# Layer-norm sums with the activations stationary and two columns of ones, and half of the output's stores on ScalarE's queue

## The chip, the cores and the metric

The kernel runs on one core of a Trainium2 chip. The metric is device microseconds (us) of one execution, median of several runs. Five engines share the core's memory: TensorE (PE in the profile; its weight loads are listed as PEld), VectorE (DVE), ScalarE (ACT), GpSimd (POOL) and SyncE (SP), which here only issues transfers. Each engine works through its own instructions in a fixed order and waits on semaphores for the others.

## The reference

Two layers of an encoder on 256 tokens of 2048 features. The first layer's mixer holds the convolution module whose layer norm is changed; the last operation of the program is an RMS norm whose result is stored.

```python
def layer_norm(x, g, b, eps=LN_EPS):
    mu = jnp.mean(xf, axis=-1, keepdims=True)
    var = jnp.mean(jnp.square(xf - mu), axis=-1, keepdims=True)
    y = (xf - mu) * lax.rsqrt(var + eps) * g.astype(jnp.float32) + b.astype(jnp.float32)
...
def conformer_conv(val, gate, dw, db, ln_g, ln_b):
    h = val * jax.nn.sigmoid(gate)
    h = depthwise_conv(h, dw, db)          # 31 taps, 1024 channels
    h = layer_norm(h, ln_g, ln_b)
    return jax.nn.silu(h)
...
    return jnp.concatenate([a_out, b_out], axis=-1) @ w_out
...
    return rms_norm(x, final_g)            # end of the program
```

The mean and the variance of a token run over the 1024 channels of the convolution.

## The kernel before

**The stream of weights.** Nearly the whole program is one stream of 960 weight tiles of 128x1024 f32 (512 KB). For each, SP loads `raw`, ScalarE rounds it to `hi` (L223), VectorE computes the rest `lo` (L225), and TensorE multiplies with both: `lin_ws` (L263, L264) holds the weights stationary, `lin_xs` (L298) holds the activations stationary. `raw` has four buffers, `hi` and `lo` three each, so that the conversion can run a few tiles ahead of TensorE and no more.

**Side work.** What isn't in that stream (the convolution, its layer norm, preparing the state-space parameters) is written as generators in `self.side`. After each weight tile `background` plays steps of the first generator as far as its credit goes: `self.rate` is added per tile, and each `yield` costs what it names. A generator that costs less ends after fewer tiles, and the next one starts sooner. `conv_ln` is followed by `s5_w1`: 32 rounds of six VectorE products (L865), with 1.5 MB of transfers each round by POOL's and SP's queues.

**The convolution's layer norm** lies with channels on partitions: `ac` is [128 channels, 8 groups, 256 tokens]. To sum over channels, a 128x128 matrix of ones is the stationary operand (`lhsT`) and `ac` moves through in eight matmuls of 256 columns (L537): every row of `pm` then holds the sums of all 256 tokens, already spread over the 128 partitions. The same is done with the squares (L545). The mean, the variance and the three Newton steps of the reciprocal root (`rsqrt_steps`) are therefore done on 128x256 tiles. Then ScalarE applies Silu (L555) and the result is split into `ao` for the output projection.

**Where it runs.** The program text has all eight attention heads first, then `mem_kv(0)`, whose weight tiles play `conv_ln`. A scheduler that simulates the program in time decides the final order on each engine; so the heads, the weight tiles of `mem_kv(0)` and the steps of the layer norm stand interleaved. PSUM tiles for small products come from two tags of two buffers, "ps" and "pt"; `pst` gives them in turn where no tag is named. In a tag, a new tile waits until the tile two before it in program order is read. The heads name theirs: scores on "ps"; `ps_wT`, `ps_o` and `ps_oT` on "pt".

**`bcast_rows`** (L140 to L146) makes a row [128, 256] out of a value per token: VectorE scales the identity by it (`dg`, L144, twice 128x128), TensorE multiplies ones with `dg` (L145, twice 128x128), VectorE copies the result (L146).

**The end.** In `ffn(1)`, L713 to L730, the two halves of 128 tokens (`tb`) are finished one after the other: sum of squares, reciprocal root, and four slices of 512 features, scaled on VectorE (slices 0 and 3, L729 and L725) or on ScalarE (1 and 2, L727), each stored by SP (L730).

Of the kernel before, what the change touches and what calls it, by code (L numbers as in the profile page):

```python
# [12 lines left out]
F32 = mybir.dt.float32  # L13
F32R = mybir.dt.float32r
I32 = mybir.dt.int32
AF = mybir.ActivationFunctionType
ALU = mybir.AluOpType
# [5 lines left out]
NTOK = 256  # L23
# [6 lines left out]
LN_EPS = 1e-5  # L30
# [4 lines left out]
class Build:  # L35
# [485 lines left out]
    def conv_ln(self, hp, ac, cdw, cv, tmp):  # L521

        nc, S = self.nc, self.S
        mu, rln, lni, lnt = tmp
        for ct in range(8):
            nc.vector.tensor_scalar(ac[:, ct, :], hp[:, ct, 0:NTOK], cdw[:, ct, 0:1], cv[:, 0, ct : ct + 1], op0=ALU.mult, op1=ALU.add)
            yield 0.4
            for j in range(1, 31):
                nc.vector.scalar_tensor_tensor(ac[:, ct, :], hp[:, ct, j : j + NTOK], cdw[:, ct, j : j + 1], ac[:, ct, :], op0=ALU.mult, op1=ALU.add)  # L529
                yield 0.4  # L530
        half = [slice(0, 4), slice(4, 8)]
        sh = [128, 4, NTOK]
        pm = self.pst("ps_ln")
        pv = pm[:, NTOK:]
        pm = pm[:, :NTOK]
        for ct in range(8):
            nc.tensor.matmul(pm, lhsT=self.ones, rhs=ac[:, ct, :], start=ct == 0, stop=ct == 7)  # L537
        nc.vector.tensor_scalar(mu, pm, 1.0 / 1024, None, op0=ALU.mult)
        sq = S.tile([128, 8, NTOK], F32, tag="A0", name="sq")
        for h in half:  # L540
            nc.vector.tensor_tensor(ac[:, h], ac[:, h], mu.unsqueeze(1).broadcast_to(sh), op=ALU.subtract)
            nc.scalar.activation(sq[:, h], ac[:, h], AF.Square)
            yield 1.2
        for ct in range(8):
            nc.tensor.matmul(pv, lhsT=self.ones, rhs=sq[:, ct, :], start=ct == 0, stop=ct == 7)  # L545
        nc.vector.tensor_scalar(mu, pv, 1.0 / 1024, LN_EPS, op0=ALU.mult, op1=ALU.add)
        yield from self.rsqrt_steps(rln, mu, lni.bitcast(I32), lnt, 1.2)
        ao = self.ao = S.tile([128, 2, 8, NTOK], F32R, tag="A0", name="ao")
        for h in half:
            nc.vector.tensor_tensor(ac[:, h], ac[:, h], rln.unsqueeze(1).broadcast_to(sh), op=ALU.mult)  # L550
            yield 1.1
        for ct in range(0, 8, 2):
            c2 = slice(ct, ct + 2)
            for i in range(ct, ct + 2):
                nc.scalar.activation(ac[:, i, :], ac[:, i, :], AF.Silu, bias=cv[:, 2, i : i + 1], scale=cv[:, 1, i : i + 1])  # L555
            self.split(ao[:, 0, c2], ao[:, 1, c2], ac[:, c2])
            yield 0.6
# [86 lines left out]
    def ffn(self, layer):  # L644
        nc, a, M, S = self.nc, self.a, self.M, self.S
# [66 lines left out]
        for tb in range(2):  # L712
            x = self.xslice(3)[tb]  # L713
            nc.vector.tensor_tensor(x, x, ps[tb], op=ALU.add)
            junk = self.R.tile([128, 512], F32, tag="junk", name="junk", bufs=1)
            nc.scalar.activation(junk, x, AF.Square, accum_out=self.ss[:, tb, 3:4])
            v = self.R.tile([128, 1], F32, tag="fv", name="fv")
            r = self.R.tile([128, 1], F32, tag="fr", name="fr")
            nc.vector.tensor_reduce(v, self.ss[:, tb], axis=AX.X, op=ALU.add)
            nc.vector.tensor_scalar(v, v, 1.0 / D, RMS_EPS, op0=ALU.mult, op1=ALU.add)  # L720
            self.rsqrt(r, v, [128, 1], "fs")
            for n in range(4):
                x = self.xslice(n)[tb]
                if n == 3:
                    nc.vector.scalar_tensor_tensor(x, x, r, fg[:, 1536:2048], op0=ALU.mult, op1=ALU.mult)  # L725
                elif n:
                    nc.scalar.activation(x, x, AF.Copy, scale=r)  # L727
                else:
                    nc.vector.tensor_scalar(x, x, r, None, op0=ALU.mult)  # L729
                nc.sync.dma_start(self.out[tb, :, n * 512 : n * 512 + 512], x)  # L730


    def s5_params(self):
# [535 lines left out]
```

## Time and profile before

| what | us |
|---|---|
| median of 3 runs (2898.27 to 2898.61) | 2898.45 |
| the profiled execution | 2897.15 |
| its span in the trace | 2895.0 |
| TensorE busy | 2854.1 (99%) |
| VectorE busy | 2203.7 (76%) |
| ScalarE busy | 1492.3 (52%) |

Busy time of TensorE is the union of its matmuls, whose ends are modelled: two matmuls that follow each other overlap in the listing, so the cost of one in a row of many is the distance of their starts and not their duration. The profiled execution is 2.15 us longer than its span, which is launch and end around it. "idle before" is time in which an engine had nothing running, followed by what ended it.

### The profile page before, as it was taken

How to read it: one execution, taken by the hardware profiler on the slowest of the kernel's cores; microseconds unless marked ns; L12 is line 12 of the kernel's file. 1: busy time of each engine (PE TensorE's matmuls, PEld its weight loads, DVE VectorE, ACT ScalarE, POOL GpSimd, SP SyncE). 2: the span in 40 equal slices, each digit the busy share in tenths (PEclk: the TensorE clock that was granted, in tenths of full speed). 3: DMA queues.
4: the chain of work that ended last, by engine and by line, in shares of the span. 5: the costliest groups of instructions: out<-in, count | busy, mean ns of one | idle time of the engine just before them, and what ended most of it. 6: DMA issues, size and time to landing. Idle time of an engine off the chain costs nothing. (4 is left out here: it accounts for less than half of the span.)

```text
span 2895.0 us, 44267 instructions
## 1 busy us (share of the span) xinstructions
PE 2854.1 (99%) x16673; PEld 2411.6 (83%) x16673; DVE 2203.7 (76%) x3524; ACT 1492.3 (52%) x2015; POOL 265.3 (9%) x504
## 2 busy tenths in 40 slices
PE   8999999999999999999999999999999999999998
PEld 7888887888888888888886787788888888888887
DVE  8899987877899887889855994556567776467765
ACT  6455554454555543455544544555455555345543
POOL 1000112222210102020201021000000000000000
PEclk9999999999999999999999999999999999999999
DMA  8655669978986788777887787655455555555554
GB/s 292 230 176 195 203 223 320 300 247 286 300 298 233 243 276 267 250 256 233 281 286 282 271 338 273 211 189 182 163 193 193 189 190 190 195 189 189 187 192 160
DMA packets 207143, 678.34 MB, mean 234 GB/s; under 512 B 33521, under 2 KB 36337, under 8 KB 206417
## 3 DMA queue, kind: packets, MB, share of 16 engines
q1 hardware_dynamic: 178592, 598.17, 61.1%
q0 software_dynamic: 28192, 76.83, 8.0%
q8 instruction: 130, 2.13, 0.3%
q14 instruction: 85, 0.69, 0.1%
q10 hardware_dynamic: 144, 0.52, 0.1%
HBM read 624.67 MB, written 61.08 MB: 237 GB/s over the span
## 5 line engine op out<-in xcount | busy, mean ns | idle before, releaser
L225 DVE TENSOR_TENSOR lo<-raw,hi 128x1024 fp32r<-128x1024 f32 x960 | 1173.1, 1223 | 534.6 <-ACT hi L223 530.9
L223 ACT CAST hi<-raw 128x1024 fp32r<-128x1024 f32 x960 | 1008.5, 1051 | 964.4 <-PE ps_xs L298 429.0
L263 PE MATMUL ps_ws<-x,hi 128*128 128x512 f32 x4352 | 1350.7, 396 | 8.0 <-DVE x L177 7.4
L264 PEld LDWEIGHTS ps_ws<-x,lo 128*128 128x128 f32 x4352 | 793.3, 188 | 191.4 <-DVE lo L225 14.8
L264 PE MATMUL ps_ws<-x,lo 128*128 128x256 f32 x4352 | 846.2, 280 | 8.1 <-DVE lo L225 7.7
L263 PEld LDWEIGHTS ps_ws<-x,hi 128*128 128x128 f32 x4352 | 674.3, 189 | 21.9 <-DVE x L177 7.4
L298 PE MATMUL ps_xs<-hi,hb 128*128 128x512 f32 x1328 | 356.5, 389 | 0.0
L298 PEld LDWEIGHTS ps_xs<-hi,hb 128*128 128x128 f32 x1328 | 249.1, 188 | 51.8
L298 PE MATMUL ps_xs<-lo,hb 128*128 128x512 f32 x664 | 204.8, 390 | 0.0
L298 PE MATMUL ps_xs<-hi,x 128*128 128x512 f32 x640 | 177.3, 394 | 1.9 <-ACT hi L223 1.9
L872 POOL DMA_DIRECT2D w1s<-d_pw x256 | 122.4, 486 | 589.5 <-DVE w1s L865 271.6
L298 PEld LDWEIGHTS ps_xs<-lo,hb 128*128 128x128 f32 x664 | 124.4, 188 | 25.9
L298 PEld LDWEIGHTS ps_xs<-hi,x 128*128 128x128 f32 x640 | 119.1, 188 | 31.6 <-issue 5.5
L298 PE MATMUL ps_xs<-hi,oT 128*128 128x512 f32 x512 | 141.1, 392 | 0.8 <-ACT hi L223 0.8
L298 PE MATMUL ps_xs<-hi,gT 128*128 128x512 f32 x512 | 138.1, 391 | 0.3 <-ACT hi L223 0.3
L271 ACT COPY z<-ps_ws 128x512 f32<-128x512 f32 x88 | 51.6, 587 | 145.2 <-PE ps_ws L263 145.2
L298 PEld LDWEIGHTS ps_xs<-hi,gT 128*128 128x128 f32 x512 | 95.6, 188 | 21.1 <-issue 0.8
L676 ACT ACTIVATE c<-z,fdb,fdw 128x256 f32<-128x256 f32 x176 | 96.3, 595 | 30.5 <-DVE z L671 30.4
L298 PEld LDWEIGHTS ps_xs<-hi,oT 128*128 128x128 f32 x512 | 95.3, 188 | 20.1 <-ACT hi L223 1.0
L529 DVE SCALAR_TENSOR_TENSOR av<-hpt,cdw,av 128x256 f32<-128x256 f32 x240 | 109.9, 484 | 0.7
L272 DVE TENSOR_TENSOR z<-ps_ws,z 128x512 f32<-128x512 f32 x88 | 60.7, 690 | 56.0 <-ACT z L271 55.7
L298 PE MATMUL ps_xs<-lo,x 128*128 128x512 f32 x320 | 100.8, 394 | 0.0
(288 smaller groups left out, 2582.0 us busy)
## 6 DMA issues: line engine op xcount, KB each, us to landing
raw<-ffn_w_up SPq DMA_DIRECT2D x352, 512.0 KB, 3.6
raw<-ffn_w_down SPq DMA_DIRECT2D x176, 512.0 KB, 4.3
raw<-xa_wv SPq DMA_DIRECT2D x64, 512.0 KB, 4.1
raw<-xa_wk SPq DMA_DIRECT2D x64, 512.0 KB, 4.4
raw<-xa_wq SPq DMA_DIRECT2D x64, 512.0 KB, 4.3
raw<-xa_wo SPq DMA_DIRECT2D x64, 512.0 KB, 3.7
raw<-ab_w_in SPq DMA_DIRECT2D x63, 512.0 KB, 3.7
w1s<-d_pw POOLq DMA_DIRECT2D x256, 64.0 KB, 5.4
```

Of the source, the lines that this page charges most:

```text
L223: nc.scalar.copy(hi, raw)
L225: ins = nc.vector.tensor_tensor(lo, raw, hi.bitcast(F32), op=ALU.subtract)
L263: both = lambda c: nc.tensor.matmul(ps[:, c], lhsT=hi[:, kk, sl[c]], rhs=x2, start=first, stop=last)
L264: low = lambda c: nc.tensor.matmul(ps[:, c, 1], lhsT=lo[:, kk, sl[c]], rhs=xh, start=False, stop=False)
L271: self.nc.scalar.copy(out, ps[:, :, 1])
L272: self.nc.vector.tensor_tensor(out, ps[:, :, 0], out, op=ALU.add)
L298: ins = mm()
L529: nc.vector.scalar_tensor_tensor(ac[:, ct, :], hp[:, ct, j : j + NTOK], cdw[:, ct, j : j + 1], ac[:, ct, :], op0=ALU.mult, op1=ALU.add)
L676: nc.scalar.activation(c[:, i], zt[:, i, 1 : NTOK + 1], AF.Identity, bias=fdb[:, ft : ft + 1], scale=w(1))
L872: nc.gpsimd.dma_start(pw[t * 16 : t * 16 + 16], self.d_pw[t, k * 4 : k * 4 + 4].partition_broadcast(16))
```

## The change

```diff
@@ conv_ln
         pm = self.pst("ps_ln")
-        pv = pm[:, NTOK:]
-        pm = pm[:, :NTOK]
-        for ct in range(8):
-            nc.tensor.matmul(pm, lhsT=self.ones, rhs=ac[:, ct, :], start=ct == 0, stop=ct == 7)
-        nc.vector.tensor_scalar(mu, pm, 1.0 / 1024, None, op0=ALU.mult)
+
+        def sums(src, o):
+            for tb in range(2):
+                for ct in range(8):
+                    nc.tensor.matmul(pm[:, o + tb * 2 : o + tb * 2 + 2], lhsT=src[:, ct, tb * 128 : tb * 128 + 128], rhs=self.ones[:, 0:2], start=ct == 0, stop=ct == 7)
+
+        sums(ac, 0)
+        cm = self.R.tile([128, 2], F32, tag="lnm", name="lnm")
+        nc.vector.tensor_scalar(cm, pm[:, 0:4:2], 1.0 / 1024, None, op0=ALU.mult)
+        self.bcast_rows(mu, cm)
         sq = S.tile([128, 8, NTOK], F32, tag="A0", name="sq")
...
-        for ct in range(8):
-            nc.tensor.matmul(pv, lhsT=self.ones, rhs=sq[:, ct, :], start=ct == 0, stop=ct == 7)
-        nc.vector.tensor_scalar(mu, pv, 1.0 / 1024, LN_EPS, op0=ALU.mult, op1=ALU.add)
-        yield from self.rsqrt_steps(rln, mu, lni.bitcast(I32), lnt, 1.2)
+        sums(sq, 4)
+        cm = self.R.tile([128, 2], F32, tag="lnm", name="lnv")
+        nc.vector.tensor_scalar(cm, pm[:, 4:8:2], 1.0 / 1024, LN_EPS, op0=ALU.mult, op1=ALU.add)
+        cr = self.R.tile([128, 2], F32, tag="lnr", name="lnr")
+        self.rsqrt(cr, cm, [128, 2], "ln")
+        yield 1.2
+        self.bcast_rows(rln, cr)
@@ ffn, end
-                nc.sync.dma_start(self.out[tb, :, n * 512 : n * 512 + 512], x)
+                (nc.scalar if n in (1, 2) else nc.sync).dma_start(self.out[tb, :, n * 512 : n * 512 + 512], x)
```

The activations are now the stationary operand and two columns of ones move: 16 matmuls of 2 columns for each of the two sums (the new L538), and the sums come out token by token, one token to a partition. Mean, variance and root are computed on 128x2 tiles, and `bcast_rows` is called twice to bring them back to rows. The generator's credit falls by 2.4 (one `yield 1.2` in place of three).

The steps move in the scheduled order. On TensorE, before, the first sum stands between an attention product (`ps_o`) and the weight products of `mem_kv(0)` (`ps_ws`), and the second sum 18 rows below it:

```order
L264 MATMUL ps_ws<-x_2391,lo 128x256
L480 MATMUL ps_o<-av,wT 128x128 x4
L537 MATMUL ps_ln<-av,ones 128x256 x8
L264 MATMUL ps_ws<-x_2391,lo 128x256
L263 MATMUL ps_ws<-x_2391,hi 128x512 x2
```

In the changed program the first sum stands at the same place, and the mean's broadcast (`ps_rb`, tag "pt") stands 178 rows below it, behind the transposes of the last head (`ps_oT`):

```order
L264 MATMUL ps_ws<-x_2406,lo 128x256
L493 MATMUL ps_oT<-ident,on 128x128 x2
L145 MATMUL ps_rb<-dg,ones 128x128 x2
L264 MATMUL ps_ws<-x_2406,lo 128x256
L263 MATMUL ps_ws<-x_2406,hi 128x512 x2
L263 MATMUL ps_ws<-x_2361,hi 128x512 x2
```

The sum of squares follows 18 and 25 rows further (4 and 12 matmuls), and the broadcast of the reciprocal root 18 rows after that, in the output projection's first tiles (`ps_xs<-..,bo`). From the mean on, the layer norm has moved from the middle of `mem_kv(0)` to its end.

On ScalarE, before, the eight Silu steps (L555) stand in one piece between two roundings of a weight tile (L223):

```order
L223 CAST hi<-raw 128x1024
L555 ACT_TABLE_LOAD
L555 ACTIVATE av<-av,cv 128x256 x8
L310 CAST ao<-av 128x512
L223 CAST hi<-raw 128x1024
L310 CAST ao<-av 128x512 x2
L223 CAST hi<-raw 128x1024
```

In the changed program they stand later, beside the output projection's tiles, in three pieces with one rounding after the first four:

```order
L563 ACT_TABLE_LOAD
L563 ACTIVATE av<-av,cv 128x256 x4
L223 CAST hi<-raw 128x1024
L563 ACTIVATE av<-av,cv 128x256
L310 CAST ao<-av 128x512
L563 ACTIVATE av<-av,cv 128x256 x3
L310 CAST ao<-av 128x512
L223 CAST hi<-raw 128x1024
L310 CAST ao<-av 128x512 x2
```

On VectorE the first step of `s5_w1` stands behind 127 `lo` tiles (130 before) and the last behind 274 (277 before): the state-space preparation with its transfers has moved three weight tiles up. The loads of keys and values (`kvraw`) stay behind 160 to 163 weight tiles.

At the end of the program ScalarE has, before, the sum of squares (L716) and two scaled slices (L727) for each half:

```order
L716 ACTIVATE junk,ss<-X 128x512
L727 ACTIVATE X<-X,fr 128x512 x2
L716 ACTIVATE junk,ss<-X 128x512
L727 ACTIVATE X<-X,fr 128x512 x2
L1265 UNCONDITIONAL_BRANCH
```

In the changed program the stores of these slices follow, those of the first half behind the second half's sum of squares:

```order
L724 ACTIVATE junk,ss<-X 128x512
L735 ACTIVATE X<-X,fr 128x512 x2
L724 ACTIVATE junk,ss<-X 128x512
L738 DMA out<-X 128x512 x2
L735 ACTIVATE X<-X,fr 128x512 x2
L738 DMA out<-X 128x512 x2
L1273 UNCONDITIONAL_BRANCH
```

SP keeps four of its eight stores.

## Rows read from the trace of the kernel before

**Rows 1.** The page: busy time, share of the span and instructions of each engine; then the granted TensorE clock (in tenths of full speed) in 40 slices.

```profile
PE 2854.1 (99%) x16673; PEld 2411.6 (83%) x16673; DVE 2203.7 (76%) x3524; ACT 1492.3 (52%) x2015; POOL 265.3 (9%) x504
...
PEclk9999999999999999999999999999999999999999
```

**Rows 2.** Busy time by stretch, from where the layer norm stands to the end of the output projection (from and to, length, then us busy and instructions for PE, PEld, DVE, ACT, POOL, then granted clock, DMA share, GB/s).

```profile
360.00:390.00 30.00, 30.00 (x174) 26.53 (x173) 25.27 (x60) 16.46 (x34) 0.00 (x0) 1.00 0.50 167
390.00:400.00 10.00, 8.64 (x50) 7.23 (x49) 7.41 (x20) 9.99 (x18) 0.00 (x0) 1.00 0.64 197
400.00:447.00 47.00, 47.00 (x277) 41.18 (x276) 42.20 (x68) 21.67 (x30) 15.26 (x32) 1.00 0.89 295
447.00:470.00 23.00, 22.91 (x100) 18.31 (x99) 16.98 (x21) 9.01 (x9) 5.91 (x13) 1.00 0.98 327
470.00:550.00 80.00, 74.95 (x337) 59.23 (x336) 65.64 (x85) 38.49 (x53) 20.81 (x44) 1.00 0.96 307
```

**Rows 3.** TensorE in order of time around the attention product and the two sums (start, length, engine, line, operation, count); consecutive matmuls of a kind are merged.

```profile
363.93 1.06 PE L480 MATMUL ps_o<-av,wT 128*128 128x128 f32 x8
364.82 3.62 PE L537 MATMUL ps_ln<-av,ones 128*128 128x256 f32 x16
368.09 0.47 PE L264 MATMUL ps_ws<-x,lo 128*128 128x256 f32 x1
...
374.46 3.62 PE L545 MATMUL ps_ln<-sq,ones 128*128 128x256 f32 x16
377.73 0.59 PE L264 MATMUL ps_ws<-x,lo 128*128 128x256 f32 x2
```

**Rows 4.** Small matmuls elsewhere: weight loads of 128x128 for matmuls of 8 columns (L1034), the second and the third of four with what follows and then the load of the next product; and a block of 32 matmuls of 16 columns whose stationary operand has 32 columns (L969), with what follows.

```profile
1526.98 0.30 PEld L1034 LDWEIGHTS ps_rr<-r,sel 128*128 128x128 f32 x2
1527.09 0.30 PEld L1034 LDWEIGHTS ps_rr<-r,sel 128*128 128x128 f32 x2
1527.31 0.19 PEld L298 LDWEIGHTS ps_xs<-hi,x 128*128 128x128 f32 x1
...
1042.87 0.47 PE L969 MATMUL ps_k<-w2s 128*32 128x16 f32 x32
1043.27 0.72 PE L298 MATMUL ps_xs<-lo,hb 128*128 128x512 f32 x2
```

**Rows 5.** VectorE: steps of the layer norm on 128x1024 and 128x256 (ns min/median/max), a step on 128x2 in the attention, and the two VectorE parts of `bcast_rows`.

```profile
L550 DVE TENSOR_TENSOR av<-av,hpt x2: 1218/1218/1219, 386.6 to 387.7; 128x1024 f32<-128x1024 f32 x2
L119 DVE TENSOR_TENSOR hpt<-hpt x3: 424/425/426, 379.8 to 384.3; 128x256 f32<-128x256 f32 x3
L110 DVE TENSOR_SCALAR hpt<-hpt x1: 293/293/293, 378.6 to 378.6; 128x256 int32<-128x256 int32 x1
L110 DVE TENSOR_SCALAR rsq_i<-so x8: 159/162/170, 235.8 to 411.0; 128x2 int32<-128x2 int32 x8
L144 DVE TENSOR_SCALAR dg<-ident,rstd x10: 279/282/289, 42.5 to 2160.3; 128x128 f32<-128x128 f32 x10
L146 DVE COPY rb<-ps_rb x5: 417/419/425, 47.2 to 2164.8; 128x256 f32<-128x256 f32 x5
```

**Rows 6.** ScalarE in order of time between two roundings of a weight tile, and TensorE where it waits behind them.

```profile
388.53 1.05 ACT L223 CAST hi<-raw 128x1024 fp32r<-128x1024 f32 x1
389.60 1.28 ACT L555 ACT_TABLE_LOAD   x1
390.90 4.05 ACT L555 ACTIVATE av<-av,cv 128x256 f32<-128x256 f32 x8
394.86 0.60 ACT L310 CAST ao<-av 128x512 fp32r<-128x512 f32 x1
395.37 1.05 ACT L223 CAST hi<-raw 128x1024 fp32r<-128x1024 f32 x1
...
397.73 0.51 PE L264 MATMUL ps_ws<-x,lo 128*128 128x256 f32 x2 [1.36 <-DVE lo L225]
```

**Rows 7.** TensorE: the output projection's first product and the first that reads `ao`.

```profile
447.02 0.62 PE L298 MATMUL ps_xs<-hi,bo 128*128 128x512 f32 x2
...
469.47 0.62 PE L298 MATMUL ps_xs<-hi,ao 128*128 128x512 f32 x2
```

**Rows 8.** Busy time and granted clock (columns as in rows 2) where the clock fell.

```profile
1534.00:1536.00 2.00, 0.67 (x3) 0.21 (x2) 1.50 (x3) 0.52 (x1) 0.00 (x0) 1.00 0.29 117
1536.00:1537.00 1.00, 0.42 (x1) 0.35 (x2) 1.00 (x2) 0.79 (x2) 0.00 (x0) 0.89 0.07 29
1537.00:1540.00 3.00, 0.71 (x3) 0.06 (x1) 3.00 (x6) 0.78 (x1) 0.00 (x0) 0.50 0.01 3
1540.00:1543.00 3.00, 3.00 (x15) 3.00 (x16) 3.00 (x3) 0.59 (x1) 0.00 (x0) 0.50 0.34 93
1543.00:1544.00 1.00, 1.00 (x6) 0.92 (x6) 1.00 (x3) 0.34 (x1) 0.00 (x0) 0.70 0.73 262
```

**Rows 9.** The end of the program: ScalarE's last scaled slices and the first two of SP's last four stores in order of time; then busy time in the stretch in which the last four move (columns as in rows 2).

```profile
2888.40 1.33 ACT L727 ACTIVATE X<-X,fr 128x512 f32<-128x512 f32 x2 [2.31 <-DVE fr L120]
2888.92 0.81 SPq L730 DMA_DIRECT2D out<-X  x2
...
2889.60:2893.00 3.40, 0.00 (x0) 0.00 (x0) 0.00 (x0) 0.14 (x1) 0.00 (x0) 0.50 0.93 309
```

## The prediction

> **What bounds the kernel now.** I read the page's busy times first: TensorE is busy 99% of the span at a granted clock of 0.9 or more of 2.4 GHz in every slice, VectorE 76%, ScalarE 52% [rows 1]. So a microsecond counts only if TensorE's own stream grows or shrinks, if TensorE waits at another place, or if it lies ahead of the first or behind the last product. Next I read the busy times by stretch from the layer norm to the end of the output projection [rows 2]: TensorE has no gap from 360 to 390 and from 400 to 447 us, loses 1.36 us from 390 to 400, next to nothing from 447 to 470, and 5.05 us from 470 to 550. In the last two stretches the DMA engines are 0.98 and 0.96 busy: there the weight tiles come late, because the state-space preparation loads and stores beside them. Then come TensorE's order of time around the two sums [rows 3], small matmuls elsewhere that show what the new ones may cost [rows 4], and ScalarE ahead of the wait of 1.36 us [rows 6].
>
> **TensorE's own work.** A matmul on f32 is listed as two: the eight of a sum stand as x16. From the first sum's start to the next product it is 368.09 - 364.82 = 3.27 us, for the second 377.73 - 374.46 = 3.27 [rows 3]. Removed: 6.54 us, all of it on the path, since TensorE has no gap there. Added: 2 sums x 16 matmuls x 2 = 64 listed matmuls of 2 columns, each with its own load of a 128x128 stationary operand. The trace has none of 2 columns. The nearest are those of 8 columns with 128x128 loads (L1034): their loads start 1527.09 - 1526.98 = 0.11 us apart, and from there to the next product it is 0.22 us for two [rows 4]. That is also the spacing of the attention product with 128 columns, (364.82 - 363.93) / 8 = 0.11 [rows 3]. Sixteen times fewer columns change nothing there, so the load of 128 columns sets the price, and with 2 columns it should again. 64 x 0.11 = 7.04 us. The other end: 32 matmuls of 16 columns with loads of only 32 columns take 1043.27 - 1042.87 = 0.40 us, 0.0125 each [rows 4]; at that price the two sums are 0.80 us. I take 7.04, as the row with the same load.
>
> The Trainium skill, "TensorE: Matmul & The Clock Gate", section "Back-to-back issue gap", gives about 60 cycles (25 ns) between isolated matmuls of up to 64 columns; by that the 64 would be 1.6 us. The same page's section "LDWEIGHTS (loading the stationary operand)" has the load time grow with the columns loaded, 107 ns for 128; by that they would be 6.8 us. The trace sides with the second, 0.11 us at 8 columns [rows 4].
>
> Two calls of `bcast_rows` add 2 x 2 matmuls of 128 columns, eight listed ones at 0.11: 0.89 us. TensorE's work: 7.04 + 0.89 - 6.54 = +1.39 us; at the low end 0.80 + 0.89 - 6.54 = -4.85.
>
> **VectorE.** It loses 14 steps on 128x256: three at 0.29 and eleven at about 0.425 us [rows 5], 5.55 us. It gains 14 on 128x2 at about 0.16, four `dg` at 0.28 and two copies at 0.42 [rows 5]: 2.24 + 1.12 + 0.84 = 4.2 us. The 1.35 us saved is counted at nothing: where the old steps stand TensorE is busy 30.00 of 30 us [rows 2]. Without that cover it would be worth at most those 1.35 us.
>
> **What moves.** The mean's broadcast waits for a PSUM buffer of the heads' tag, and in the order of the changed program it stands 178 rows below the first sum. So squares, root, Silu and `ao` move from 368-400 us to about 430-465. Three things follow.
>
> First, the wait of 1.36 us goes. Before, ScalarE loads its table (1.28), does eight Silu steps (4.05) and one rounding of `ao` (0.60) between two weight tiles, 5.9 us in all, and TensorE then waits for `lo` [rows 6]. What is late next at that place is nothing in the rows: the heads and the weight tiles alone keep TensorE full from 400 to 447 [rows 2].
>
> Second, the same steps come again from 447 on, where DMA is 0.98 busy and fewer tiles are ready ahead. They are now cut by a rounding after four of the eight. The ends: nothing, if ScalarE's 14 free microseconds of 23 there hide it [rows 2]; 5.05 us, if it doubles what TensorE loses from 470 to 550. I take 1.4 us, since the nearest row is the same burst's own wait.
>
> Third, added waits in TensorE's fixed order. At the mean's broadcast nothing is awaited, its `dg` is made tens of microseconds earlier. Between the sum of squares and the root's broadcast VectorE does 13 small steps, a `lo` tile, a step of `s5_w1` and two `dg`: 13 x 0.16 + 1.2 + 0.7 + 0.56 = 4.5 us (the `lo` tile taken as long as L550, the other an estimate of half that). TensorE has 20 products of `mem_kv` and 19 of the output projection meanwhile: 20 x 0.17 (47.0 / 277 from 400 to 447 [rows 2]) + 19 x 0.23 (22.45 us from the first `bo` to the first `ao`, 8 weight tiles of 12 products [rows 7]) = 7.8 us. That leaves 3.3 us of room, and if VectorE is later than that, the whole output projection stands behind the waiting broadcast. From there to the first product on `ao` are 67 products, 15.4 us. Copy, two scalings, table, Silu, one rounding in between and the split need about 0.42 + 2.44 + 1.28 + 4.05 + 1.05 + 0.60 + 0.7 (an estimate for the last) = 10.5 us [rows 5, 6]. So `ao` is in time by some 5 us.
>
> The state-space preparation starts and ends three weight tiles earlier, which I count at nothing. It brings the same bytes beside the same weight stream, and the loads of keys and values still meet it.
>
> **The end.** The second half's four stores move 1 MB from 2889.60 to 2893.00 with the DMA engines 0.93 busy [rows 9]. So issuing them earlier or from two queues can win at most 0.07 x 3.4 = 0.24 us, unless the first of them goes out earlier, and that one (slice 0, at 2888.92) waits for VectorE and stays on SP. ScalarE's two stores of the first half stand behind the sum of squares, in the 2.31 us that it idles before `fr` [rows 9]; uncovered, two issues are 0.81 us. I take -0.2 us, with ends -0.24 and +0.81.
>
> The Trainium skill, "DMA: Bandwidth & Descriptors", section "Issuing engines are not separate DMA queues", says that transfers started from several engines run on the same 16 DMA engines and that only time on the issuing sequencer is saved. The 0.93 agrees [rows 9]. If queues were separate the stores would win up to the half of 3.4 us.
>
> **The sum.** +1.39 - 1.36 + 1.4 - 0.2 = +1.23 us. Against the profiled execution, 2897.15 us (a span of 2895.0 and 2.15 around it): 2898.4. The median of the runs shown is 1.30 us above that execution, so the forecast is 2898.45 + 1.23 = 2899.7 us, an increase of 0.04%.
>
> **The rivals.**
>
> *The columns set the price* (the 64 matmuls at 0.0125 us): -4.85 - 1.36 + 1.4 - 0.2 = -5.0, 2893.4 us. For it speaks only a row with loads of 32 columns, against it L1034 [rows 4]. By the skill's isolated gap, named above, it would be 2894.2.
>
> *The clock falls in the sums.* TensorE's granted clock went to 0.50 (1.2 GHz) shortly before 1537 us and came back after 1543.5, some 6.8 us, after 0.67 busy microseconds in two and then single products [rows 8]. In the new sums the array takes 2 columns in 0.11 us for 3.5 us on end, which may look as idle. A fall of that length over a dense stream costs half, 3.4 us: 2903.1 with one, 2906.5 with two. Two decide for slower. Against it: the loads go on throughout, and every stretch with small products and waits in rows 2 shows 1.00.
>
> *The layer norm comes too late* (the slower side). Place: 447 to 470 us. VectorE and ScalarE work in order, so a weight tile that DMA brings late holds up the root and the Silu steps behind it. TensorE then waits at the broadcast once the 3.3 us of room are used, and again for roundings behind the burst. Price: 5.05 in place of 1.4, and about 2.3 us (a rounding, 1.05, and a `lo`, 1.2) at the broadcast: +1.39 - 1.36 + 5.05 + 2.3 - 0.2 = +7.2, 2905.6 us. For it speaks DMA at 0.98; against it that TensorE lost only 0.09 us there [rows 2].
>
> *The shift of three tiles frees the crowded stretch*: the 5.05 us from 470 to 550 mostly go: 2894.6. Nothing in the rows asks for it; the transfers are the same.
>
> **How the numbers follow.** A measurement of this kernel can tell about 0.2%, 5.8 us, from no change: faster is below 2892.6, slower above 2904.3. Forecast 0.57; columns 0.08; clock 0.14, half of it with two falls; late layer norm 0.15; freed stretch 0.06. Faster takes half of the first rival and a little of the last: 0.05. Slower takes two falls (0.07) and most of the late layer norm (0.10): 0.17. Within 0.2%: 0.78. The outer bounds add up to -4.85 - 1.36 - 0.24 = -6.45 (2892.0) and, with the stretch doubled, stores uncovered and two falls, +1.39 - 1.36 + 5.05 + 0.81 + 6.8 = +12.7 (2911.2). The range 2893.8 to 2906.6 leaves out no more than 2 in 10.
>
> **What would show it.** In the new profile: the sums' listed matmuls start 0.11 us apart (right) or far less (columns); granted clock 1.00 through both sums, or 0.50 behind them; no wait near 397 us; TensorE's waits from 447 to 470 about 1.4 us, and none at the root's broadcast; the last stores still at a DMA share above 0.9, their end within 0.3 us of where it was, counted from the last product. The prediction is wrong if TensorE's summed waits between 360 and 690 us change by more than 4 us, or if the clock falls there.

## Result and the profile after

The changed kernel takes 2911.16 us (median of 5, 2908.14 to 2913.46) against 2898.61 us before (2898.27 to 2901.63): a ratio of 1.0043 with a 95% interval of 1.003 to 1.0056, 12.6 us more. The forecast was 2899.7 us with a range to 2906.6, so it was wrong, and on the side of "slower", to which it gave 0.17. Run again beside some of the experiments, the changed kernel took 2907.83 us against 2898.79 (ratio 1.003, 1.0018 to 1.0042): 9 to 12.6 us is what has to be explained. A trace is one execution of a kernel whose executions lie several us apart, so costs go by medians here, and traces are read for where time goes.

The page of the changed kernel, busy times and granted clock, which answers to [rows 1]:

```profile
PE 2867.0 (98%) x16713; PEld 2421.6 (83%) x16713; DVE 2201.6 (76%) x3530; ACT 1493.2 (51%) x2015; POOL 265.6 (9%) x504
...
PEclk9999999999999999999999999999999999999999
```

The span is 2911.7 us against 2895.0, so TensorE idles 44.7 us in place of 40.9. Only 3.8 us of 16.7 are waits; TensorE itself is busy 12.9 us longer with 40 more listed matmuls. The clock's line shows nothing, since one of its 40 slices is 73 us long. The mean of the granted clock shows it (span and clock of the core, of the changed kernel and then of the kernel before):

```profile
core 0: 2911.7 us, clock 0.995
```

```profile
core 0: 2895.0 us, clock 0.998
```

0.003 of 2900 us is 8.7 us (the clock is given to three digits, so 6 to 12). It isn't this execution alone: the mean granted clock of the five runs is 0.994. In the second comparison it is 0.9950 over the six runs of the changed kernel and 0.9973 over the 25 of the kernel before, which is 6.6 of the 9 us. The stretches tell where. Busy time by stretch, columns as in [rows 2]:

```profile
365.50:369.00 3.50, 3.50 (x34) 3.50 (x33) 0.86 (x6) 2.34 (x12) 0.00 (x0) 1.00 0.45 153
369.00:373.00 4.00, 4.00 (x16) 3.43 (x16) 2.93 (x13) 1.04 (x1) 0.00 (x0) 0.57 0.00 0
...
390.00:400.00 10.00, 10.00 (x58) 8.72 (x57) 9.39 (x20) 4.80 (x7) 1.48 (x4) 1.00 0.67 222
400.00:441.00 41.00, 39.37 (x233) 34.25 (x231) 33.13 (x55) 17.64 (x26) 13.77 (x29) 1.00 0.92 279
441.00:444.50 3.50, 2.40 (x16) 2.12 (x17) 3.50 (x6) 1.74 (x3) 0.00 (x0) 0.97 1.03 337
444.50:454.50 10.00, 10.00 (x41) 9.33 (x40) 6.22 (x14) 2.56 (x3) 3.81 (x8) 0.50 0.80 257
454.50:470.00 15.50, 15.50 (x74) 12.95 (x73) 14.49 (x25) 10.14 (x15) 2.62 (x6) 1.00 0.86 272
```

The first sum fills 365.5 to 369.0. Right behind it, with no wait at all, the clock is at 0.57 for 4 us, so at half (1.2 GHz) for 3.4 of them: 1.7 us lost. From 444.5 to 454.5 it is at half all along: 5 us. Other falls begin at about 506 and 622 us, each behind a wait. In the trace of the kernel before none stands ahead of 1536 us. That isn't so in each of its executions: in the kernel with the stores alone (the first experiment), which is the same up to there, a fall stands at 606.6, behind a wait of 1.85 us:

```profile
606.60:610.00 3.40, 3.40 (x16) 3.21 (x16) 2.22 (x4) 2.45 (x4) 0.00 (x0) 0.50 0.14 54
```

TensorE in order of time, at the two sums and their broadcasts, the first product on `bo`, the first and the last on `ao`, a product of the cross attention that waits, and the program's last product; it answers to [rows 3, 6, 7]:

```profile
365.52 3.63 PE L538 MATMUL ps_ln<-ones,av 128*128 128x2 f32 x32
369.01 0.38 PE L264 MATMUL ps_ws<-x,lo 128*128 128x256 f32 x1
...
432.61 0.61 PE L145 MATMUL ps_rb<-dg,ones 128*128 128x128 f32 x4
441.37 1.05 PE L538 MATMUL ps_ln<-ones,sq 128*128 128x2 f32 x8 [2.00 <-ACT sq L547]
443.15 0.51 PE L264 MATMUL ps_ws<-x,lo 128*128 128x256 f32 x2 [0.72 <-DVE lo L225]
446.20 5.11 PE L538 MATMUL ps_ln<-ones,sq 128*128 128x2 f32 x24
456.30 0.62 PE L298 MATMUL ps_xs<-hi,bo 128*128 128x512 f32 x2
460.62 0.61 PE L145 MATMUL ps_rb<-dg,ones 128*128 128x128 f32 x4
...
476.27 0.62 PE L298 MATMUL ps_xs<-hi,ao 128*128 128x512 f32 x2
...
553.82 0.62 PE L298 MATMUL ps_xs<-hi,ao 128*128 128x512 f32 x2
...
620.20 0.39 PE L602 MATMUL ps_xs<-kT,qT 128*128 128x256 f32 x1 [2.92 <-ACT qT L310]
...
2900.96 0.39 PE L301 MATMUL ps_e<-hi,hb 128*128 128x512 f32 x1
```

and the last of these two in the kernel before:

```profile
545.19 0.61 PE L298 MATMUL ps_xs<-hi,ao 128*128 128x512 f32 x2
...
602.63 0.39 PE L594 MATMUL ps_xs<-kT,qT 128*128 128x256 f32 x1 [1.31 <-ACT qT L310]
```

The first product on `bo` is at 456.30 against 447.02 [rows 7]: 9.3 us are lost by there. The last on `ao` is 8.6 us late. Counting weight products (L263, L264 and L298) through both traces, the changed kernel is then 12.4 us late at the one that stands at 622 us before, 16.4 at the one at 806 us, and 16.8 at the program's last product. Its second trace is 9.0, 10.8 and 12.0 us late at the same three.

Why TensorE waits at the sum of squares is read on VectorE and then ScalarE, in order of time:

```profile
435.47 0.47 DVE L495 SCALAR_TENSOR_TENSOR bo<-ps_oT,sub_g,bo 128x256 fp32r<-128x256 f32 x1
438.40 0.69 DVE L873 TENSOR_TENSOR w1t<-w1s 128x512 f32<-128x512 f32 x1 [2.46 <-DMA w1s<-s_b]
439.01 2.35 DVE L546 TENSOR_TENSOR av<-av,hpt 128x1024 f32<-128x1024 f32 x2
```

```profile
440.26 1.06 ACT L547 ACTIVATE sq<-av 128x1024 f32<-128x1024 f32 x1 [2.90 <-DVE av L546]
```

A product of the state-space preparation stands in VectorE's queue ahead of the layer norm's subtraction, and VectorE idles 2.46 us until that product's operand has come. The subtraction, the squares and the sum of squares all wait behind it.

### The profile page after: what moved, and what is told of

The parts are those of the page before. It is cut to its first block, busy times and chain, and to the rows that moved or that the text cites. A ratio compares the mean times of both kernels' runs of the same rounds, so it can differ in the third digit from the quotient of the medians.

```text
span 2911.7 us, 44337 instructions
## 1 busy us (share of the span) xinstructions
PE 2867.0 (98%) x16713; PEld 2421.6 (83%) x16713; DVE 2201.6 (76%) x3530; ACT 1493.2 (51%) x2015; POOL 265.6 (9%) x504
## 5 line engine op out<-in xcount | busy, mean ns | idle before, releaser
L223 ACT CAST hi<-raw 128x1024 fp32r<-128x1024 f32 x960 | 1008.5, 1051 | 975.5 <-PE ps_xs L298 399.1
L263 PE MATMUL ps_ws<-x,hi 128*128 128x512 f32 x4352 | 1355.6, 397 | 8.9 <-DVE x L177 7.3
L264 PEld LDWEIGHTS ps_ws<-x,lo 128*128 128x128 f32 x4352 | 795.6, 189 | 194.9 <-DVE lo L225 16.6
L264 PE MATMUL ps_ws<-x,lo 128*128 128x256 f32 x4352 | 849.1, 281 | 9.0 <-DVE lo L225 8.9
L263 PEld LDWEIGHTS ps_ws<-x,hi 128*128 128x128 f32 x4352 | 676.7, 189 | 23.1 <-DVE x L177 7.3
L298 PE MATMUL ps_xs<-hi,hb 128*128 128x512 f32 x1328 | 357.0, 390 | 0.0
L298 PEld LDWEIGHTS ps_xs<-hi,hb 128*128 128x128 f32 x1328 | 249.0, 188 | 51.8
L298 PE MATMUL ps_xs<-lo,hb 128*128 128x512 f32 x664 | 204.8, 390 | 0.0
L298 PE MATMUL ps_xs<-hi,x 128*128 128x512 f32 x640 | 177.0, 393 | 1.1 <-ACT hi L223 1.1
L298 PEld LDWEIGHTS ps_xs<-lo,hb 128*128 128x128 f32 x664 | 124.5, 188 | 25.9 <-issue 0.2
L298 PEld LDWEIGHTS ps_xs<-hi,x 128*128 128x128 f32 x640 | 119.1, 188 | 30.8 <-issue 5.1
L298 PE MATMUL ps_xs<-hi,oT 128*128 128x512 f32 x512 | 140.9, 392 | 0.8 <-ACT hi L223 0.8
L298 PE MATMUL ps_xs<-hi,gT 128*128 128x512 f32 x512 | 138.1, 391 | 0.3 <-ACT hi L223 0.3
L298 PEld LDWEIGHTS ps_xs<-hi,gT 128*128 128x128 f32 x512 | 95.7, 188 | 21.1 <-issue 0.8
L298 PEld LDWEIGHTS ps_xs<-hi,oT 128*128 128x128 f32 x512 | 95.4, 188 | 20.2 <-ACT hi L223 1.0
L298 PE MATMUL ps_xs<-lo,x 128*128 128x512 f32 x320 | 100.7, 394 | 0.0
```

Of the source, the lines that this page charges most:

```text
L223: nc.scalar.copy(hi, raw)
L263: both = lambda c: nc.tensor.matmul(ps[:, c], lhsT=hi[:, kk, sl[c]], rhs=x2, start=first, stop=last)
L264: low = lambda c: nc.tensor.matmul(ps[:, c, 1], lhsT=lo[:, kk, sl[c]], rhs=xh, start=False, stop=False)
L298: ins = mm()
```

## Experiments

Each kernel was timed beside the kernel before, whose median was then 2897.9 to 2898.8 us; a ratio is against that median, with its 95% interval. "Credit" is the generator's cost that decides at which weight tile the state-space preparation starts: lowered (as in the change), it starts three tiles early.

**The stores alone**, on the kernel before.

```diff
-                nc.sync.dma_start(self.out[tb, :, n * 512 : n * 512 + 512], x)
+                (nc.scalar if n in (1, 2) else nc.sync).dma_start(self.out[tb, :, n * 512 : n * 512 + 512], x)
```

> The kernel before with only the stores changed (slices 1 and 2 on ScalarE's queue). All theories put the loss into the layer norm and what follows it, so the time stays at the kernel before's, 2898.5 us within 1 us, and the last four stores still move with a DMA share above 0.9. If the stores cost or win something, it shows here alone: more than 1 us either way would mean that.

2898.24 us, ratio 0.9999 (0.999 to 1.0009). The stores have no part in it.

**The layer norm's place put back.** `bcast_rows` takes the PSUM tag "ps", so that it needn't wait for the heads' "pt"; first with the credit lowered, then as before, then with 128 columns of ones as well (the diff leaves out how the tag passes through `bcast_rows` and, with 128 columns, the new places of the sums in `pm`).

```diff
@@ all three
-        self.bcast_rows(mu, cm)
+        self.bcast_rows(mu, cm, "ps")
...
-        self.bcast_rows(rln, cr)
+        self.bcast_rows(rln, cr, "ps")
@@ second and third
-        yield 1.2
+        yield 3.6
@@ third
-                    nc.tensor.matmul(pm[:, o + tb * 2 : o + tb * 2 + 2], lhsT=src[:, ct, tb * 128 : tb * 128 + 128], rhs=self.ones[:, 0:2], start=ct == 0, stop=ct == 7)
+                    nc.tensor.matmul(pm[:, o + tb * 128 : o + tb * 128 + 128], lhsT=src[:, ct, tb * 128 : tb * 128 + 128], rhs=self.ones, start=ct == 0, stop=ct == 7)
```

> The change with only the place put back (broadcasts from the scores' tag); the generator's credit is 2.4 lower as in the change, so the state-space preparation is three weight tiles earlier. Shift theory (some 4 to 7 us of the loss between 470 and 870 us come from the shifted transfers): 4 to 7 us above the run with place and credit put back, about 2908 us. Place theory: no difference to that run, within 1.5 us.

> The change with two things put back: the broadcasts take their PSUM buffer from the tag of the scores, so that the layer norm stands early again, and the generator costs as much credit as before, so that the state-space preparation isn't shifted. Sums still of 2 columns. Clock theory (a stream of 2-column matmuls lets the granted clock fall): the clock falls after both sums, 3.4 us at half each, so +1.4 us of work and +3.4 us for the clock: about 2903 us. Place theory (the loss comes only from the late place in the crowded stretch and the waits there): clock 1.00, about 2900 us.

> As the run before (early place, old credit), with 128 columns of ones moving instead of 2. Clock theory: same spacing of 0.11 us, since the loads set it, but the granted clock stays at 1.00 through both sums, so about 2900 us, 3 us below the run with 2 columns. If the loads or the small accumulations were what lowers the clock, it falls here too and the time equals that run's.

2906.03 us (ratio 1.003, 1.0017 to 1.0044), 2904.13 (1.002, 1.0011 to 1.0029) and 2902.72 (1.0015, 1.0005 to 1.0024). The place gives back 2 us against the second timing of the changed kernel and 5 against the first, the credit 1.9 more, the columns 1.4 more. The 2 us and the last two steps are inside the intervals. The clock behind the first sum, with 2 columns and then with 128 (columns as in rows 2):

```profile
369.00:373.00 4.00, 4.00 (x15) 3.41 (x15) 2.98 (x13) 1.04 (x1) 0.00 (x0) 0.57 0.00 0
```

```profile
369.00:373.00 4.00, 4.00 (x25) 3.49 (x24) 3.33 (x15) 1.57 (x4) 0.00 (x0) 1.00 0.00 0
```

In the same 4 us the one runs 15 matmuls, the other 25. In both kernels with 2 columns a second fall stands right behind the second sum (from 389.3 and 389.6 us), with no wait ahead of it; with 128 columns there is none.

**The clock by itself.** Into the kernel before, behind its own first sum, 16 matmuls with activations stationary whose result is not used; 2 columns move in one kernel (shown), 128 in the other. Either burst also moves later steps in the order, in both kernels alike, so the pair compares cleanly, and each of them with the kernel before does not.

```diff
+        for tb in range(2):
+            for ct in range(8):
+                nc.tensor.matmul(pv[:, 0:2], lhsT=ac[:, ct, tb * 128 : tb * 128 + 128], rhs=self.ones[:, 0:2], start=ct == 0, stop=ct == 7)
```

> The kernel before, its own sums untouched, and behind the first of them 16 matmuls of 2 columns with activations stationary, into the half of the PSUM tile that the squares fill later (their result is not used). Both theories: 32 listed matmuls 0.11 us apart, 3.5 us, from the product ahead to the product behind. Theory A (two columns bring the clock down): granted clock about 0.5 to 0.6 for 3.4 us right behind them, so 3.5 + 1.7 = 5.2 us more between two weight products on either side, 2903.3 from 2898.1. Rival (the clock falls by waits and not by columns): clock 1.00, 3.5 us, 2901.6.

> As the burst of two columns, with 128 columns of ones moving. Both theories: the same spacing of 0.11 us and clock 1.00 throughout: 3.5 us more between two weight products on either side, 2901.6. If the clock falls here too, it is the burst's kind (many loads, a stationary operand of activations, f32) and not its two columns.

2905.74 us (ratio 1.0028, 1.0018 to 1.0037) and 2902.87 (1.0019, 1.0009 to 1.0028). TensorE in order of time at the burst, and busy time and clock behind it, with 2 columns:

```profile
368.70 3.63 PE L540 MATMUL ps_ln<-ones,av 128*128 128x2 f32 x32
372.19 0.36 PE L264 MATMUL ps_ws<-x,lo 128*128 128x256 f32 x1
```

```profile
373.00:377.00 4.00, 4.00 (x19) 3.48 (x18) 3.72 (x4) 3.33 (x5) 0.00 (x0) 0.57 0.00 0
```

and with 128:

```profile
368.86 3.73 PE L540 MATMUL ps_ln<-ones,av 128*128 128x128 f32 x32
372.35 0.36 PE L264 MATMUL ps_ws<-x,lo 128*128 128x256 f32 x1
```

```profile
373.00:377.00 4.00, 4.00 (x26) 3.51 (x25) 3.95 (x5) 3.70 (x5) 0.00 (x0) 1.00 0.00 0
```

Both bursts take 3.49 us to the next product, at the same place, with TensorE busy and loading throughout and no wait. Only the moving columns differ, and only the two columns are followed by half clock. That the clock falls because of them is shown: a fall stands at the end of the first two-column stream in all six traces that have one (it begins in the stream's last 2.2 us or within 0.9 us behind it), and in none of the other ten traces is there a fall from 360 to 380 us, five of them with 96 or 128 columns at this place. The fall behind one burst costs 0.43 x 4 = 1.7 us. The medians differ by 2.9 us, more than that, and their intervals overlap. The mean granted clock of the ten runs of each is 0.9958 and 0.9972, some 4 us of 2900, so the clock alone can make the difference; why it is more than one fall isn't shown.

**The columns of the change**, place and credit as in it: 128, then 96. With 128 the order shifts too: the mean's broadcast and the squares stand 62 and 64 listed products earlier than in the change. With 96 the places up to the sum of squares are those of the change. The diff shows 96 columns and leaves out the new places of the sums in `pm`.

```diff
-                    nc.tensor.matmul(pm[:, o + tb * 2 : o + tb * 2 + 2], lhsT=src[:, ct, tb * 128 : tb * 128 + 128], rhs=self.ones[:, 0:2], start=ct == 0, stop=ct == 7)
+                    nc.tensor.matmul(pm[:, o + tb * 128 : o + tb * 128 + 96], lhsT=src[:, ct, tb * 128 : tb * 128 + 128], rhs=self.ones[:, 0:96], start=ct == 0, stop=ct == 7)
```

> The change with 128 columns of ones moving in place of 2, all else as it is: the layer norm stays late and the state-space preparation three tiles early. Theory A (the two-column sums themselves bring the clock down, and the longest fall of the changed kernel, 10.2 us at 444.5, was begun by the second sum): no fall behind the first sum, none or one of 3.4 us at the second; 3.41 x 0.5 + 10.24 x 0.5 = 6.8 us less than the changed kernel's 2911.2, about 2904.4. Theory B (the wait of 2.0 us ahead of the second sum begins that fall, whatever the columns): the fall of some 10 us stays, only the first goes, about 2909.5. Rival C (the clock has no share, the late place costs by its waits): 2911 with or without falls.

> The change with 96 columns of ones moving in both sums. Unlike the kernel with 128, this one keeps the layer norm's places on TensorE up to the sum of squares and the last head's transposes where the changed kernel has them (behind the same weight products); only the root's broadcast comes 28 rows later. Theory A (few moving columns bring the clock down): no fall behind the first sum (1.7 us back) and none or a short one at the sum of squares (3.4 to 5.1 us back): 2904.4 to 2906.1. Theory P (the place decides: VectorE waits for a transfer of the state-space preparation, and TensorE behind it at the sum of squares): that wait of about 2 us and a fall behind it stay, 2909.5 to 2911.

> The changed kernel once more, beside the others on the same chip. If its time is a matter of the order and the clock: again 2909 to 2913, a fall of 3.4 us right behind the first sum, and a longer one at the sum of squares behind a wait of some 2 us. If the profiled execution was an odd one: the long fall at the sum of squares is missing, or the median lies near 2905.

2904.14 us (ratio 1.0022, 1.0013 to 1.0031) with 128; 2906.53 (1.0033, 1.0022 to 1.0044) with 96, beside 2907.83 for the changed kernel in the same comparison. TensorE at the sum of squares, and its first product on `bo`, with 96 columns:

```profile
439.43 1.13 PE L538 MATMUL ps_ln<-ones,sq 128*128 128x96 f32 x8 [2.01 <-ACT sq L547]
441.21 0.80 PE L264 MATMUL ps_ws<-x,lo 128*128 128x256 f32 x2 [0.65 <-DVE lo L225]
444.83 2.81 PE L538 MATMUL ps_ln<-ones,sq 128*128 128x96 f32 x24
450.99 0.61 PE L298 MATMUL ps_xs<-hi,bo 128*128 128x512 f32 x2
```

and in the changed kernel run again:

```profile
440.82 1.05 PE L538 MATMUL ps_ln<-ones,sq 128*128 128x2 f32 x8 [0.40 <-ACT sq L547]
442.60 0.51 PE L264 MATMUL ps_ws<-x,lo 128*128 128x256 f32 x2 [0.73 <-DVE lo L225]
446.28 2.81 PE L538 MATMUL ps_ln<-ones,sq 128*128 128x2 f32 x24
454.09 0.62 PE L298 MATMUL ps_xs<-hi,bo 128*128 128x512 f32 x2
```

The wait ahead of the squares' sum belongs to the place and not to the columns: with 96 it is as long as in the first trace of the changed kernel (2.01 and 2.00). It differs between executions (0.40 in the second trace). With 96 columns, too, the clock falls behind it, for 3.4 us from 440.9. There the output projection starts 3.1 and 5.3 us earlier than in the two traces of the changed kernel, by less time at half clock, and yet the median is only 1.3 us better. In its trace the falls from 499 to 622 us, behind waits of 1.54 to 4.80 us, last 13.7 us in all, against 6.8 in the first trace of the changed kernel and 3.4 in the second. The second has its falls spread otherwise (6.8 us behind the first sum, twice 3.4 at the second), so the long one of the first trace is one case of several. As far as these runs tell, a gain at the sums is mostly lost later.

**The credit of the change put back**, two columns and late layer norm kept; then with 128 columns too.

```diff
@@ both
-        yield 1.2
+        yield 3.6
@@ second, also
-rhs=self.ones[:, 0:2]
+rhs=self.ones
```

> The change with the generator's credit as before (3.6 in place of 1.2), so that the state-space preparation starts at the weight tile where it started before; two columns, the layer norm late. If the shift of three tiles costs something: the 1.9 us by which the early-placed pair (2906.0 with the shift, 2904.1 without) differed come off, about 2909. If its cost lies in the collision of the late layer norm with that preparation's transfers (the VectorE product that waited 2.46 us for its DMA ahead of the sum of squares in the changed kernel): that wait goes, with it the wait of 2.0 us at the sum and the long fall, 2904 to 2906. If the shift is nothing: 2911.

> The change with both remedies that the runs so far pointed at: 128 columns of ones move in place of 2, and the generator's credit is as before. In the kernel with the credit alone put back (2901.0) the clock stood at half for 6.83 us behind the first sum and 3.41 us behind the second, 5.1 us of work; with the columns it should stand at full in both. If the two causes add up: 2901.0 - 5.1 = 2895.9, no slower than the kernel before. If what the columns give back at the sums is lost again in the crowded stretch behind (as the kernel with 96 columns did): 2899 to 2901.

2901.03 us (ratio 1.0008, 0.9998 to 1.0017) and 2902.06 (1.001, 1.0001 to 1.0019). The first is the largest step of all: one number takes back 7 to 10 us of the 9 to 12.6. Most of that is clock: its mean over the ten runs is 0.9968 against 0.994 and 0.9950 of the changed kernel, 5 to 8 us. And the collision at the squares is gone. From 420 to 452 us, a stretch that holds the second sum and ends at the output projection, TensorE now waits for nothing, and the clock is at half for some 3 us of it (10 us in the first trace of the changed kernel):

```profile
420.00:452.00 32.00, 32.00 (x192) 28.43 (x191) 29.21 (x51) 15.99 (x20) 10.49 (x22) 0.95 0.93 301
```

The two remedies don't add up: 2895.9 was expected if they did. With both, the mean clock is 0.9973, as in the kernel before (0.9972), so little of the 4.2 us that stay can be clock. Clock across the first sum (columns as in rows 2) and TensorE at the first product on `bo` and the last on `ao`, with the credit alone:

```profile
365.00:375.00 10.00, 10.00 (x54) 9.28 (x54) 4.14 (x21) 3.81 (x13) 0.00 (x0) 0.66 0.20 60
...
460.00:560.00 100.00, 94.68 (x437) 76.64 (x436) 81.33 (x104) 48.09 (x67) 28.82 (x61) 1.00 0.98 316
```

```profile
451.94 0.62 PE L298 MATMUL ps_xs<-hi,bo 128*128 128x512 f32 x2
...
549.48 0.61 PE L298 MATMUL ps_xs<-hi,ao 128*128 128x512 f32 x2
```

and with the columns too:

```profile
365.00:375.00 10.00, 10.00 (x73) 9.29 (x72) 6.16 (x25) 5.86 (x17) 0.00 (x0) 1.00 0.32 107
...
460.00:560.00 100.00, 90.71 (x413) 71.78 (x412) 77.27 (x100) 46.06 (x64) 24.55 (x53) 1.00 0.96 301
```

```profile
447.30 0.62 PE L298 MATMUL ps_xs<-hi,bo 128*128 128x512 f32 x2
...
549.17 0.62 PE L298 MATMUL ps_xs<-hi,ao 128*128 128x512 f32 x2
```

With full clock the output projection starts 4.6 us earlier and ends 0.3 us earlier. In between DMA is 0.96 busy or more in both, and TensorE idles 9.3 us of 100 in place of 5.3. As these two traces read, the projection ends when its weights have come, and time saved ahead of it turns into waits inside it.

**The shift alone**, on the kernel before with its own sums: the credit lowered by 2.4 as in the change, and raised by 2.4.

```diff
-        yield from self.rsqrt_steps(rln, mu, lni.bitcast(I32), lnt, 1.2)
+        yield from self.rsqrt_steps(rln, mu, lni.bitcast(I32), lnt, 0.4)
```

(2.0 in place of 0.4 in the second.)

> The kernel before with the generator's credit lowered by 2.4 and nothing else: its own sums of 256 columns, its layer norm early, but the state-space preparation three weight tiles early and the last head's transposes moved down, as in the changed kernel. If that shift costs by itself what the changed kernel with the credit put back gained (2911.2 - 2901.0 = 10.2): 2908.8. If it costs what the early-placed pair differed by (1.9): 2900.5. If it costs only together with a late layer norm: 2898.6.

> The kernel before with the generator's credit raised by 2.4 and nothing else, so that the state-space preparation starts two to three weight tiles later (132 in place of 130) instead of earlier (127, which took 2901.5). If earlier costs because more of the preparation meets the loads of the weight stream and the last heads, later should win about as much: 2896. If the place it has is only one of several, each with its own collisions: 2898 to 2902.

2901.54 us (ratio 1.001, 1.0 to 1.0019) and 2901.8 (1.0013, 1.0004 to 1.0022): 2.8 and 3.9 us more, the first at the edge of what is told from nothing. The win expected of a later start didn't come, so nothing here says that it is earliness as such that costs. One thing shows in every kernel with the credit lowered: the first product on `qT` of one head waits for ScalarE 2.55 to 4.80 us (six traces: the changed kernel twice, 96 and 128 columns, place put back, shift alone), against 0.20 to 1.85 us in those with the credit as before or raised. ScalarE, and TensorE behind it, in order of time in the kernel with the shift alone:

```profile
607.51 1.04 ACT L223 CAST hi<-raw 128x1024 fp32r<-128x1024 f32 x1 [6.53 <-DMA raw<-xa_wq]
608.47 0.61 ACT L310 CAST qT<-qs 128x512 fp32r<-128x512 f32 x1
```

```profile
609.13 0.58 PE L594 MATMUL ps_xs<-kT,qT 128*128 128x256 f32 x1 [2.73 <-ACT qT L310]
```

The rounding of `qT` stands behind that of a weight tile, and ScalarE idles 6.5 us until that tile's transfer has come. The clock falls at such a wait in five of the six. But it falls in this part of the program, behind a wait of 1.85 to 2.20 us, in four of the other ten traces too. So some 1.5 us of wait go with the shift, and of the fall's 1.7 us only a part; whether that is what the shift alone costs isn't shown.

**Toward a faster kernel**: the kernel before, with the squares and a second tile of ones rounded to the weight products' type for the second sum.

```diff
+        self.ones_r = C.tile([128, 128], F32R, name="ones_r")
+        nc.vector.tensor_copy(self.ones_r, self.ones)
...
-        sq = S.tile([128, 8, NTOK], F32, tag="A0", name="sq")
+        sq = S.tile([128, 8, NTOK], F32R, tag="A0", name="sq")
...
-            nc.tensor.matmul(pv, lhsT=self.ones, rhs=sq[:, ct, :], start=ct == 0, stop=ct == 7)
+            nc.tensor.matmul(pv, lhsT=self.ones_r, rhs=sq[:, ct, :], start=ct == 0, stop=ct == 7)
```

> The kernel before with the squares and a second tile of ones rounded to the type of the weight products (the mean's sum stays in full f32): the eight matmuls of the sum of squares take one pass each. By the weight products of 256 columns of that type (about 0.115 us each) 0.9 us in place of 3.27, 2.35 us off TensorE's path: 2896.3 from 2898.6. Against it: the layer norm's steps come 2 us earlier and the order shifts, which the other runs showed to be worth 1 to 3 us either way; then 2895 to 2900.

2896.6 us, ratio 0.9996 (0.9986 to 1.0005): the forecast of this run was 2896.3, but 2 us are not told apart from no change.

## Why the prediction was wrong, point by point

*The work of the sums: right.* The first sum is 3.49 us to the next product, 0.11 us for each of 32 listed matmuls, and the columns set no price: a burst of 128 columns takes the same 3.49. The rival "the columns set the price" fell. Of the two rules of the Trainium skill weighed there ("TensorE: Matmul & The Clock Gate", sections "Back-to-back issue gap" and "LDWEIGHTS (loading the stationary operand)"), the isolated gap of 25 ns doesn't fit the spacing of 0.11 us, and the load's 107 ns does.

*The clock in the sums: the step that failed first.* The prediction gave this rival 0.14, and argued against it that the loads go on throughout and that all stretches with small products show 1.00 [rows 2]. But none of these stretches held 3.5 us of two-column products and nothing else. The loads did not hold the clock up here: both bursts load throughout, and behind them it stood at 0.57 and at 1.00. The price was mis-sized the other way: one fall of 3.4 us costs 1.7, not 3.4, since the row it was taken from was a fall of twice that length [rows 8]. Yet falls were not confined to the sums. The Trainium skill, "TensorE: Matmul & The Clock Gate", section "HAM oscillation — how this bites in real kernels", has the clock fall while TensorE waits some 3 to 5 us for transfers, and counts half of the time at the lower clock as lost. The trace agrees on the price (15 matmuls at 0.57 against 25 at 1.00 in the same 4 us), and in part on the cause: the falls at about 506 and 622 us stand behind waits, but shorter ones (2.20 and 2.92 us), and the falls right behind the sums have no idle TensorE before them.

*The added waits: a step left out.* The prediction priced VectorE's chain between the sum of squares and the root's broadcast, and that broadcast indeed waits for nothing (460.62). It did not ask what stands ahead of the squares themselves. In its list "a step of `s5_w1`" was 0.7 us of work; here VectorE stood 2.46 us at such a step, waiting for its transfer, and TensorE waited 2.00 + 0.72 us. Behind the wait came the long stretch at half clock, together with the rest of the two-column sum: 5 us lost in the first trace, 3.4 in the second. Which of the two began it isn't told apart: with 96 columns the clock fell behind the wait, and with the credit put back it fell behind the two-column sum with no wait.

*The shift of three tiles, "counted at nothing": the term that failed by most.* Alone it costs 2.8 us, at the edge of what is told from no change. With the late layer norm and the two columns, taking it back gains 7 to 10. The reason given, the same bytes beside the same stream, was beside the point: the shift changes which instruction on ScalarE and VectorE stands behind which late transfer, and the last head's place (its transposes stand 14 products on `hi` further down in the order). With the credit put back the collision at the squares is gone, and 5 to 8 us of what comes back are clock. That run also moves the squares up by 64 products, so how much of the 7 to 10 us is the collision at the squares and how much the later waits is not settled.

*The wait at 397 us, `ao`, the end: right; the Silu burst: a term too many.* The old wait is gone: TensorE is busy 10.00 us of 10 from 390 to 400. The 1.4 us for the burst in its new place did not come: 15.50 of 15.50 from 454.5 to 470, and no wait up to 480. `ao` is in time: its first product at 476.27 waits for nothing. From the start of the last product to the span's end it is 10.7 us, 10.8 before, and the stores alone changed nothing.

*The sum.* In the profiled execution: 1.33 us of work (2 x (3.49 - 3.27) + 0.89 for the broadcasts), 3.8 us of waits and some 8.5 of clock (falls of 23.9 us in all ahead of the end in place of 6.8, halved as if TensorE were busy throughout) are 13.6 of 16.7 us; the rest is not assigned. The measured median lies at the prediction's outer bound (2911.2) by chance: that sum holds a doubled stretch and uncovered stores, which did not come. The kernels with the credit put back stay 2.4 to 6 us above the kernel before, as do its own two neighbours with the credit changed (2.8 and 3.9). No kernel with another order was faster, and why was not settled. Of the two signs that the prediction named against itself, the falls of the clock between 360 and 690 us came; TensorE's waits there hardly changed (12.5 us in place of 11.4), less than the 4 it named.

## What to carry to other kernels

Where TensorE is full, price a change of its products also by what the clock makes of them: here a stream of products with two moving columns was as long as planned and still slowed what followed. Where a scheduler or a credit sets the order, follow every queue past which a step is moved to the instruction that waits for a transfer, since what stands behind that one waits too. And where a stretch is paced by DMA, as the output projection is here, a gain ahead of it may be lost in it.

## What the runs showed that was not expected

Sixteen matmuls of 2 columns, with loads of 128x128 all along, are followed by half clock, and sixteen of 128 columns at the same spacing of 0.11 us are not (0.57 and 1.00 over the same 4 us): the clock and the engine's busy time tell different things here. And moving the state-space preparation by two or three weight tiles in either direction, with no other edit, costs this kernel some 3 to 4 us, the earlier place at the edge of what is told from no change.
